# A residual kept in DRAM through the up-projections and the second mixer, its place used for split weights, and one more seven-product unit

## The chip, the cores and the metric

The kernel runs on one core of a Trainium2 chip. The metric is the device time of one execution in microseconds (us); less is better. The engines of the core work side by side, each on its own instructions in order: TensorE (PE) multiplies matrices, VectorE (DVE) and ScalarE (ACT) work element by element, GpSimd (POOL) copies and issues DMAs, SyncE (SP) issues DMAs. Semaphores make one engine wait for another.

## What is computed

A small encoder of two layers on 256 tokens with 2048 channels, in float32. Each layer is a token mixer and a gated MLP with a short convolution; the first layer's mixer is grouped-query attention with rotary positions (A), the second's is dilated sliding-window attention in three head groups (B).

```python
D_MODEL, SEQ, DEPTH, D_FF = 2048, 256, 2, 5632

def conv_ffn(h, w_up, conv_w, conv_b, w_down):
    u = h @ w_up
    ...
    gate, val = jnp.split(u, 2, axis=-1)
    return (jax.nn.silu(gate) * val) @ w_down

def reference(x, a_w_qkv, a_w_o, a_q_gain, a_k_gain, b_w_qkv, b_w_o, rel_bias,
              mix_norm, ffn_norm, w_up, conv_w, conv_b, w_down, final_norm):
    h = x
    for i in range(DEPTH):
        hn = rms_norm(h, mix_norm[i])
        j = i // N_MIXERS
        if i % N_MIXERS == 0:
            h = h + mixer_a(hn, a_w_qkv[j], a_w_o[j], a_q_gain[j], a_k_gain[j])
        else:
            h = h + mixer_b(hn, b_w_qkv[j], b_w_o[j], rel_bias)
        h = h + conv_ffn(rms_norm(h, ffn_norm[i]), w_up[i], conv_w[i], conv_b[i], w_down[i])
    return rms_norm(h, final_norm)
```

`h` is the residual: it is needed for the norm at the start of a sub-layer and for the addition at its end, and not in between.

## The kernel before

**Products.** Every weight matrix is cut into blocks of 512 rows (a group, `kg`) by 512 columns. A weight tile `raw` is half of such a block, [128, 2, 512], 512 KB, loaded by SP. To keep float32 precision, a product is made of three matmuls: ACT rounds `raw` to a high part `wh` (line 147), DVE subtracts it to get a low part `wl` (line 148), and PE multiplies high by high, high by low and low by high (lines 135 to 137). `feed` (line 117) does one block: two splits, and 4 row tiles x 2 token halves x 3 = 24 matmuls of 512 columns. `project` (line 160) does one column block of all groups. `wh` and `wl` have four buffers each (`NHL`), `raw` has four, and in some stages every third `raw` comes from one or two more places (`extra`, line 102).

**Seven-product units.** For some groups `fast_unit` (line 167) computes the four quarter products of two column blocks with seven products in place of eight, by Strassen's method. It loads four weight tiles, makes four sums of them on DVE (line 181), splits seven tiles (lines 182 and 183) and runs 7 x 6 = 42 matmuls (lines 189 to 191), where two fed blocks would take 48. The seven results go to seven or eight accumulators; `fold` (line 196) or the end of `up_pair` (line 525) adds them up on DVE. In an up-projection, pair `p` of a gate and a value block goes through `up_pair` when `p` is in `UP`: six fed blocks and one unit, for group 0. The combinations of the inputs that a unit needs (`picks`) are made once for a layer, at the end of pair 0 (`sums`, line 521).

**Stages.** Mixer A, MLP of layer 0, mixer B, MLP of layer 1. An MLP runs in two halves (`HALVES`: pairs 0 to 5, then 6 to 10). Each half first makes its pairs of up-projections, then adds its part of the down-projection to `h`: in the first half by two calls of `pair` (line 216) for the column blocks (0, 1) and (2, 3); in the second half column block 0 alone, then `pair` for (1, 2), then block 3. `pair` runs fed blocks and units in the order it is given; its `finish` adds one side to `h` (`add_residual`, line 461), and the generator `closing` adds the folds to `h` and calls `post` for each column block, where there is one. Mixer B projects two halves of heads (`hf`) for three groups each, some of them by `up_pair` (`MIX`), then the values, and ends in `out_proj` (line 894), which uses `project2` for the column blocks (0, 1) and `pair` for (2, 3).

**The residual.** `h` (line 58) is one tile [128, 2, 2048] on chip, 16 KB in each partition, for the whole run. After the last addition to a column block, `post` takes its sum of squares (`sumsq_cols`, line 368) and starts `late_transpose` (line 403), which turns the block into the inputs `hT` of the next sub-layer: transpositions on DVE, copies on POOL and ACT, splits on ACT and DVE.

**What sets the order.** Work beside the products is written as generators, which `step` (line 85) advances between blocks. The order of the text is a priority only: a scheduler orders each engine's instructions by priority and by when their inputs and buffers are free, and `tc.high_priority(offset=AHEAD)` raises the splits by 60 places. POOL issues its DMAs in the order of its own instructions; SP issues all weight loads. The output is scaled by `put` and written by `send` (lines 810 to 853) at the very end, first for the first token half, then for the second.

## Time and profile before

| | us |
|---|---|
| median of three runs | 2223.42 |
| lowest and highest of them | 2221.92, 2224.94 |
| span of the profiled execution, first to last instruction | 2220.5 |
| PE busy | 2207.1 |
| DVE busy | 1823.1 |
| ACT busy | 1528.2 |
| POOL busy | 546.1 |

Of the profiled execution the span is known, and no time of its own beside it. The mean granted clock of PE is 0.999 of full speed. The shares of busy time are means over stages of different kinds; for one stage the view of busy times by stretches is read. Stages in the trace, by the first matmul of each: the MLP of layer 0 from about 257 us, its first down-projections from 517, its second half from 643, mixer B from 964, the MLP of layer 1 from 1506, the output from 2210. In a row, PE is a matmul, DVE, ACT and POOL are those engines, "q" behind an engine is its queue; L148 is line 148; `wl<-raw,wh` is the tile written and the tiles read; x7 is a count. In the timeline the columns are the start, the duration, the engine, the line, the operation and, in brackets, the idle time before it and what ended it.

### The profile page before, as it was taken

The numbers are of one execution on the slowest core, as the hardware profiler recorded it, in microseconds if no ns is written. First come the engines' busy times: TensorE is split into PE (matmuls) and PEld (weight loads), VectorE is DVE, ScalarE is ACT, GpSimd is POOL, SyncE is SP. The second block draws the span as 40 slices with busy tenths as digits, with TensorE's granted clock in tenths as the row PEclk, the third lists the DMA queues.
The fourth block names the chain that finished last, engine by engine and source line by source line (L and its number), as shares of the span: only waits on it lengthen the run. The fifth ranks groups of instructions, "written<-read, shape, count | busy, mean of one in ns | idle before, by whom it ended". The sixth has DMA issues, their size and how long they took to land.

```text
span 2220.5 us, 28992 instructions
## 1 busy us (share of the span) xinstructions
PE 2207.1 (99%) x9933; PEld 1828.5 (82%) x9933; DVE 1823.1 (82%) x2295; ACT 1528.2 (69%) x2328; POOL 546.1 (25%) x793
## 2 busy tenths in 40 slices
PE   9999999999999999999999999999999999999998
PEld 7888888888888888888888888888888888888887
DVE  6877669899897998868876878587798998879887
ACT  7666677787457787677756775567777855678764
POOL 3343222321003221042354216003222300212211
PEclk9999999999999999999999999999999999999999
DMA  8665665656656566665666555556555565656754
GB/s 305 192 220 184 216 188 190 201 189 196 203 181 222 186 205 200 204 202 195 183 199 199 174 180 189 190 184 214 181 202 194 192 209 190 217 162 218 224 193 143
DMA packets 126181, 439.60 MB, mean 198 GB/s; under 512 B 14408, under 2 KB 18248, under 8 KB 126032
## 3 DMA queue, kind: packets, MB, share of 16 engines
q1 hardware_dynamic: 123056, 429.05, 59.2%
q0 software_dynamic: 2688, 8.39, 1.5%
q8 instruction: 78, 1.28, 0.2%
q14 instruction: 71, 0.58, 0.1%
q10 hardware_dynamic: 288, 0.30, 0.0%
HBM read 432.34 MB, written 5.34 MB: 197 GB/s over the span
## 4 chain that ended last, share of the span: by engine, by line
PE 54%; POOL 1%; issue 1%; DMA 0%; ACT 0%; DVE 0%; POOLq 0%; DVEq 0%; ACTq 0%
PE acc L136 15%; PE acc L135 15%; PE acc L137 15%; PE ps L190 1%; PE ps L189 1%; PE ps L191 1%; PE acc L190 1%; PE acc L189 1%; PE acc L191 1%; DMA raw<-in_w_b_dram 0%; POOL wide L399 0%; PE ps L1422 0%; PE ps L342 0%; POOL wide L384 0%; ACT wh L147 0%
## 5 line engine op out<-in xcount | busy, mean ns | idle before, releaser
L148 DVE TENSOR_TENSOR wl<-raw,wh 128x1024 fp32r<-128x1024 f32 (+1 forms) x700 | 858.9, 1237 | 257.6 <-ACT wh L147 253.1
L147 ACT ACTIVATE wh<-raw 128x1024 fp32r<-128x1024 f32 (+1 forms) x700 | 726.8, 1046 | 342.5 <-PE acc L137 240.6
L136 PE MATMUL acc<-wl,xh 128*128 128x512 f32 x1984 | 773.8, 390 | 1.5 <-DVE wl L148 1.4
L135 PE MATMUL acc<-wh,xh 128*128 128x512 f32 x1984 | 773.7, 390 | 0.5 <-ACT wh L147 0.5
L137 PE MATMUL acc<-wh,xh 128*128 128x512 f32 x1984 | 772.1, 389 | 0.0
L136 PEld LDWEIGHTS acc<-wl,xh 128*128 128x128 f32 x1984 | 372.6, 188 | 81.5 <-DVE wl L148 5.7
L135 PEld LDWEIGHTS acc<-wh,xh 128*128 128x128 f32 x1984 | 372.5, 188 | 77.4 <-ACT wh L147 1.0
L137 PEld LDWEIGHTS acc<-wh,xh 128*128 128x128 f32 x1984 | 372.4, 188 | 76.9
L632 POOL COPY u<-quad 32x256 f32<-32x256 f32 x352 | 237.7, 675 | 702.5 <-DVE quad L380 684.4
L135 PE MATMUL acc<-wh,a 128*128 128x512 f32 x720 | 280.9, 390 | 0.0
L136 PE MATMUL acc<-wl,a 128*128 128x512 f32 x720 | 280.3, 389 | 0.0
L137 PE MATMUL acc<-wh,a 128*128 128x512 f32 x720 | 280.0, 389 | 0.0
L182 ACT ACTIVATE wh<-raw 128x1024 fp32r<-128x1024 f32 x140 | 148.5, 1061 | 122.4 <-PE acc L137 102.6
L183 DVE TENSOR_TENSOR wl<-raw,wh 128x1024 fp32r<-128x1024 f32 x140 | 166.9, 1218 | 6.3 <-ACT wh L182 5.8
L632 ACT ACTIVATE u<-quad 32x256 f32<-32x256 f32 x352 | 147.8, 420 | 23.2 <-DVE quad L380 18.7
L137 PEld LDWEIGHTS acc<-wh,a 128*128 128x128 f32 x720 | 135.1, 188 | 28.3 <-DVE a L331 0.2
L135 PEld LDWEIGHTS acc<-wh,a 128*128 128x128 f32 x720 | 135.2, 188 | 27.7
L136 PEld LDWEIGHTS acc<-wl,a 128*128 128x128 f32 x720 | 135.2, 188 | 27.6 <-DVE wl L148 0.3
L399 POOL COPY wide<-quad 32x256 f32<-32x256 f32 x88 | 54.8, 622 | 234.8 <-DVE quad L380 167.8
L492 ACT ACTIVATE stg<-acc,rstd 128x512 f32<-128x512 f32 x122 | 81.9, 685 | 32.9 <-PE acc L137 21.3
L384 POOL COPY wide<-quad 32x256 f32<-32x256 f32 x133 | 89.8, 675 | 41.4 <-DVE quad L380 32.0
L380 DVE STREAM_TRANSPOSE quad<-stg 128x512 f32<-128x512 f32 x112 | 75.7, 696 | 11.6 <-ACT stg L492 11.4
(318 smaller groups left out, 2444.5 us busy)
## 6 DMA issues: line engine op xcount, KB each, us to landing
raw<-in_w_up_dram SPq DMA_DIRECT2D x352, 512.0 KB, 4.6
raw<-in_w_down_dram SPq DMA_DIRECT2D x176, 512.0 KB, 4.6
raw<-in_w_b_dram SPq DMA_DIRECT2D x144, 512.0 KB, 4.6
raw<-in_w_bo_dram SPq DMA_DIRECT2D x48, 512.0 KB, 4.4
raw<-in_w_a_dram SPq DMA_DIRECT2D x40, 512.0 KB, 4.7
raw<-in_w_ao_dram SPq DMA_DIRECT2D x32, 512.0 KB, 4.5
raw<-in_w_a_dram SPq DMA_DIRECT2D x16, 256.0 KB, 5.8
there<-quad POOLq DMA_DIRECT2D x6, 512.0 KB, 3.7
```

Source lines behind the costliest of these rows:

```text
L135: nc.tensor.matmul(accs[m], xh, wh[:, j, :], start=st, stop=False)
L136: nc.tensor.matmul(accs[m], xh, wl[:, j, :], start=False, stop=False)
L137: nc.tensor.matmul(accs[m], xl, wh[:, j, :], start=False, stop=sp)
L147: nc.scalar.activation(wh[:, c], r[:, c], AF.Copy)
L148: newest[0] = nc.vector.tensor_tensor(wl[:, c], r[:, c], wh[:, c].bitcast(F32), ALU.subtract)
L182: nc.scalar.activation(wh, r, AF.Copy)
L183: newest[0] = nc.vector.tensor_tensor(wl, r, wh.bitcast(F32), ALU.subtract)
L380: nc.vector.transpose(quad[:, :, at, :], src.rearrange("p (x c t) -> p c x t", c=4, t=32))
L384: nc.gpsimd.tensor_copy(o[32 * c:32 * c + 32, :, 32 * q:32 * q + 32], quad[32 * q:32 * q + 32, c])
L399: nc.gpsimd.tensor_copy(dst, src)
L492: evac[0] = nc.scalar.activation(o[:, m, :], accs[m], AF.Copy, scale=rstd[:, m:m + 1])
L632: put(u[32 * c:32 * c + 32, :, :, 32 * q:32 * q + 32], quad[32 * q:32 * q + 32, c].rearrange("p (j m) t -> p j m t", m=2))
```

## The change

`UP` gets 1 in addition, so that the second pair of the first half goes through `up_pair` in both layers. `h` becomes four tiles of [128, 2, 512], one for a column block, in four places `h0` to `h3`. `put_away` writes a column block to DRAM on the POOL queue and gives up its tile; `fetch` takes a new tile and reads it back. A block is written away when its last addition is done (in the mixers' output, in the first half of both MLPs, and in the second half of the first), and read back before the next addition. While it is away, every third split takes its `wh` and `wl` from the places of `h` (`h0` and `h2`, or `h1` and `h3`, in turn) and not from the four buffers; `more` switches this on from the end of a half's first pair to the end of its last, and in mixer B from the end of its first group to the last but one value projection. `closing` now calls `post` in the first half as well, which there is `put_away`. The writes of the output are cut at the new tiles' borders.

```diff
-UP = 2, 4, 6, 8
+UP = 1, 2, 4, 6, 8
...
-    h = hpool.tile([P, 2, D], F32, name="h")
+    h = {}
...
+    def new_h(n):
+        h[n] = hpool.tile([P, 2, 512], F32, tag=f"h{n}", name=nm("h"))
+        return h[n]
+
+    away, more, splits = {}, [False], [0]
+
+    def put_away(n):
+        if n not in away:
+            away[n] = dpool.tile([P, 2, 512], F32, name=f"away{n}")
+        nc.gpsimd.dma_start(away[n], h.pop(n))
+
+    def fetch(n):
+        if n in h:
+            return
+        nc.gpsimd.dma_start(new_h(n), away[n])
+
+    def new_split():
+        splits[0] += 1
+        i = splits[0] // 3 % 2
+        if more[0] and splits[0] % 3 == 0:
+            return [hpool.tile([P, 2, 512], F32R, tag=f"h{i + k}", name=nm(t)) for k, t in ((0, "wh"), (2, "wl"))]
+        return [spool.tile([P, 2, 512], F32R, tag=t, name=nm(t), bufs=NHL) for t in ("wh", "wl")]
...
@@ feed and fast_unit
-            wh = spool.tile([P, 2, 512], F32R, tag="wh", name=nm("wh"), bufs=NHL)
-            wl = spool.tile([P, 2, 512], F32R, tag="wl", name=nm("wl"), bufs=NHL)
+            wh, wl = new_split()
...
@@ pair
         def closing():
             yield from fold(acc, *ns, *folds())
-            for side in range(2 if post else 0):
+            for side in range(2):
                 yield
                 while side not in added:
                     yield
...
         for i, (kg, side) in enumerate(order):
             while ready is not None and kg not in ready:
                 step()
+            if i == 4:
+                fetch(ns[0])
+                fetch(ns[1])
...
@@ late_transpose
+        src = h[n]
         yield
...
@@ ffn, in the loop over pairs
                     extra[0] = fp, ["raw2"]
+                    more[0] = True
                     start(value_gen(va, value, gate, last_value))
...
+                more[0] = False
                 start(flush(last_value))
...
@@ ffn, post, second half of the first layer
                         sumsq_cols(ss, n, junk)
                         start(late_transpose(hTn, n, g_next, fp, "cg", lambda: quad_tile(fp, "quad", 2)))
+                        put_away(n)
...
@@ ffn, the output
-                    put(0, 0, 1024, "act", r)
-                    put(0, 1024, 1536, "act", r)
-                    send(0, 0, 1024, nc.sync)
-                    send(0, 1024, 2048, nc.sync)
+                    for c in range(0, 1536, 512):
+                        put(0, c, c + 512, "act", r)
+                    for c in range(0, 2048, 512):
+                        send(0, c, c + 512, nc.sync)
...
-                    put(1, 1024, 1536 + NT, "dve", r)
+                    put(1, 1024, 1536, "dve", r)
+                    put(1, 1536, 1536 + NT, "act", r)
...
@@ ffn, the down-projections of the first half
                         pair(wd, ns, slots, both[0] + both[3] + [(4, 0)] + f0 + [(4, 1), (5, 0)] + f1 + [(5, 1)], spot, folds,
-                             None, 3 * (ns[0] == 0), ready)
+                             put_away, 3 * (ns[0] == 0), ready)
...
@@ ffn, the down-projections of the second half
                 for kg in range(np_):
                     while kg not in ready:
                         step()
+                    if kg == 2:
+                        fetch(0)
...
                 pair(wd, (1, 2), slots, order, spot, folds, post, 0, ready)
+                fetch(3)
...
@@ out_proj
         def post(n):
             sumsq_cols(ss, n, junk)
             start(late_transpose(hTn, n, g_next, pool, tag, new_quad))
+            put_away(n)
...
+        for n in range(2):
+            fetch(n)
         if units:
...
@@ mixer_a
             def load_x(n):
-                nc.sync.dma_start(h[:, :, n * 512:(n + 1) * 512],
+                nc.sync.dma_start(new_h(n),
                                   x[:, n * 512:(n + 1) * 512].rearrange("(p m) c -> p m c", m=2))
...
@@ mixer_b
                     start(s_gen(g, project(w_b, ns[1], hT, kgs), kT, bts))
+                    more[0] = True
...
                 for g in range(3):
+                    more[0] = hf == 0 or g < 2
                     accs = project(w_b, 6 * g + 4 + hf, hT, kgs)
```

(The further lines of the diff put `h[n][:, m]` in the place of `h[:, m, n * 512:(n + 1) * 512]`.)

More of the change, by code (lines that the diff above doesn't have):

```diff
@@ L176, in fast_unit @@
         for i, (q, r) in enumerate(((1, b11), (2, b21), (3, b22), (5, t1), (7, b12), (6, t2), (4, t4))):
-            wh = spool.tile([P, 2, 512], F32R, tag="wh", name=nm("wh"), bufs=NHL)
-            wl = spool.tile([P, 2, 512], F32R, tag="wl", name=nm("wl"), bufs=NHL)
+            wh, wl = new_split()
             with tc.high_priority(offset=AHEAD):
@@ L197, in hs @@
         def hs(m, n):
-            return h[:, m, n * 512:(n + 1) * 512]
+            return h[n][:, m]
         tt = nc.vector.tensor_tensor
@@ L369, in sumsq_cols @@
         for m in range(2):
-            nc.scalar.activation(junk(), h[:, m, n * 512:(n + 1) * 512], AF.Square,
+            nc.scalar.activation(junk(), h[n][:, m], AF.Square,
                                  accum_out=ss[:, m, n:n + 1])
@@ L411, in late_transpose @@
             for m in range(2):
-                quad_T(quad, slice(m, 8, 2), h[:, m, n * 512:(n + 1) * 512])
+                quad_T(quad, slice(m, 8, 2), src[:, m])
             yield
@@ L422, in late_transpose @@
         space, quad_tag, wide_tag = next_space[0]
-        src = h[:, :, n * 512:(n + 1) * 512]
         quad, o = quad_tile(space, *quad_tag), wide_tile(space, *wide_tag)
@@ L462, in add_residual @@
         for m in range(2):
-            hs = h[:, m, n * 512:(n + 1) * 512]
+            hs = h[n][:, m]
             nc.vector.tensor_tensor(hs, accs[m], hs, ALU.add)
@@ L782, in post @@
                         for m in range(2):
-                            hs = h[:, m, n * 512:(n + 1) * 512]
+                            hs = h[n][:, m]
                             nc.scalar.activation(junk(), hs, AF.Square, accum_out=ss[:, m, n:n + 1])
@@ L808, in ffn, with cols @@
                 outv = out.rearrange("(p m) c -> m p c", m=2)
+                def cols(m, c0, c1):
+                    return h[c0 // 512][:, m, c0 % 512:(c1 - 1) % 512 + 1]
                 def put(m, c0, c1, how, r):
-                    hs = h[:, m, c0:c1]
+                    hs = cols(m, c0, c1)
                     if how == "fin":
@@ L819, in send @@
                 def send(m, c0, c1, eng):
-                    eng.dma_start(outv[m, :, c0:c1], h[:, m, c0:c1])
+                    eng.dma_start(outv[m, :, c0:c1], cols(m, c0, c1))
                 def first_out(acc):
-                    hs = h[:, 0, 1536:]
+                    hs = h[3][:, 0]
                     nc.vector.tensor_tensor(hs, acc, hs, ALU.add)
@@ L827, in first_out @@
                     put(0, 1536, 2048, "fin", r)
-                    put(0, 0, 1024, "act", r)
-                    put(0, 1024, 1536, "act", r)
-                    send(0, 0, 1024, nc.sync)
-                    send(0, 1024, 2048, nc.sync)
+                    for c in range(0, 1536, 512):
+                        put(0, c, c + 512, "act", r)
+                    for c in range(0, 2048, 512):
+                        send(0, c, c + 512, nc.sync)
                 def last_out(acc, parts):
-                    hs = h[:, 1, 1536:]
+                    hs = h[3][:, 1]
                     nc.vector.tensor_tensor(hs, acc, hs, ALU.add)
```

## The prediction

> **What bounds the kernel now.** I read the page first: the share of each engine, then the list of who waited for whom, then the timeline of PE alone.
>
> ```profile
> span 2220.5 us, 28992 instructions
> PE 2207.1 (99%) x9933; PEld 1828.5 (82%) x9933; DVE 1823.1 (82%) x2295; ACT 1528.2 (69%) x2328; POOL 546.1 (25%) x793
> ACT wh L147 <- PE acc L137: 240.6, 177, 2.1
> DVE wl L148 <- ACT wh L147: 253.1, 221, 3.8
> 1900.06 0.39 PE L137 MATMUL acc<-wh,xh 128*128 128x512 f32 x1
> ...
> 1905.95 0.39 PE L136 MATMUL acc<-wl,xh 128*128 128x512 f32 x1
> ```
>
> PE is busy for 99% of the span, so it is the bound. The timeline gives its pace: the two rows are 26 matmuls apart, (1905.95 - 1900.06) / 26 = 0.2265 us from start to start; the 0.39 is a modelled duration that overlaps the next one. The two waits say the rest: ACT (high parts, line 147) waits 240.6 us for PE to free a split buffer, and DVE (low parts, line 148) waits 253.1 us for ACT. The conversion mostly runs as far ahead as its four buffers allow and stands there. Only two things can then shorten the kernel: fewer matmuls, or the few places where PE waits for a low part. I looked for those as start-to-start distances over 0.227 in the stages where the change gives more split buffers:
>
> ```profile
> 377.79 0.39 PE L135 MATMUL acc<-wh,xh 128*128 128x512 f32 x1
> 378.68 0.50 PE L136 MATMUL acc<-wl,xh 128*128 128x512 f32 x1 [0.50 <-DVE wl L148]
> 487.05 0.39 PE L135 MATMUL acc<-wh,xh 128*128 128x512 f32 x1
> 487.50 0.50 PE L136 MATMUL acc<-wl,xh 128*128 128x512 f32 x1
> 1030.31 0.39 PE L189 MATMUL ps<-wh,s 128*128 128x512 f32 x1
> 1030.72 0.50 PE L190 MATMUL ps<-wl,s 128*128 128x512 f32 x1
> 1282.86 0.39 PE L189 MATMUL ps<-wh,s 128*128 128x512 f32 x1
> 1283.17 0.50 PE L190 MATMUL ps<-wl,s 128*128 128x512 f32 x1
> 1735.90 0.39 PE L135 MATMUL acc<-wh,xh 128*128 128x512 f32 x1
> 1736.25 0.50 PE L136 MATMUL acc<-wl,xh 128*128 128x512 f32 x1
> ```
>
> They lose 0.89 - 0.23 = 0.66, then 0.22, 0.18, 0.08 and 0.12 us: 1.26 us in all. So the buffers can win about 1.3 us at most, in a kernel of 2220.
>
> **The change, part by part.**
>
> *The unit.* With 1 in UP, pair 1 of the first half goes through up_pair in both layers. Two projections are 2 x 4 groups x 24 = 192 matmuls; six fed groups and a unit of 7 x 6 are 144 + 42 = 186. That is 6 fewer per layer, 12 in all, on the path: 12 x 0.2265 = **-2.72 us**. What it adds lies on DVE and ACT, and the same unit one pair later (340 to 382 us) shows its price; a view by stretches gives the room (columns: length, PE, PEld, DVE, ACT, POOL busy, clock, DMA share, GB/s).
>
> ```profile
> 296.00:340.00 44.00, 44.00 (x196) 36.44 (x195) 29.32 (x38) 35.90 (x55) 14.97 (x24) 1.00 0.62 189
> 340.00:382.00 42.00, 41.50 (x183) 33.72 (x182) 37.06 (x43) 31.07 (x47) 9.11 (x12) 1.00 0.54 178
> 426.00:468.00 42.00, 42.00 (x187) 34.75 (x187) 37.10 (x40) 31.01 (x44) 8.88 (x15) 1.00 0.58 198
> 468.00:512.00 44.00, 43.94 (x194) 35.91 (x193) 42.06 (x63) 36.42 (x58) 14.62 (x18) 1.00 0.60 196
> L183 DVE TENSOR_TENSOR wl<-raw,wh 128x1024 fp32r<-128x1024 f32 x7 | 8.2, 1218 | 0.0
> L181 DVE TENSOR_TENSOR raw<-raw,raw 128x1024 f32<-128x1024 f32 x4 | 4.9, 1225 | 0.1
> L551 DVE TENSOR_TENSOR acc<-acc,junk 128x512 f32<-128x512 f32 x1 | 0.7, 690 | 0.0
> L182 ACT ACTIVATE wh<-raw 128x1024 fp32r<-128x1024 f32 x7 | 7.4, 1059 | 4.9 <-PE acc L137 4.4 <-PE ps L191 0.3 <-PE acc L191 0.2
> 374.19 2.01 ACT L147 ACTIVATE wh<-raw 128x1024 fp32r<-128x1024 f32 x2 [3.77 <-DMA raw<-in_w_up_dram]
> ```
>
> Splits go from 16 to 12 + 7 = 19. DVE gets 3 x 1.22 + 4 sums x 1.23 + 8 folds of about 0.69 = 14.1 us; ACT gets 3 x 1.06 + about 0.7 = 3.9 us. In pair 1 (296 to 340) DVE has 44 - 29.3 = 14.7 us free and ACT 8.1. It fits, but DVE is then nearly full, and no lead is built for pair 2. The unit's burst shows in pair 2: PE lost 0.66 us at 378, since ACT waited 3.77 us for a weight tile whose buffer the unit held (last row). More split buffers do not mend that. For pair 1 I bound it by 0, as in the unit of pair 4 (426 to 468, PE 42.00 of 42.00), and by 0.66 in both layers, 1.32 in all. I take half: **+0.66 us**; the range keeps both ends, with -0 below, since an added burst cannot give time back.
>
> *Split buffers in h's place.* Every third split takes one of two more pairs, so four become six in the up-projections and the second mixer. Pair 5 (468 to 512), where DVE is busy for 42.06 of 44 us, gets the lead that pair 4 can now build; its losses at 487 and 1736 and those of the second mixer at 1030 and 1283 should go: 0.22 + 0.12 + 0.18 + 0.08 = **-0.60 us**, bounded by 0 and by all 1.26. What is late next at these places is DVE itself, which then has its work done earlier.
>
> *The residual's journeys.* Per use of put_away and fetch, n from 0 to 3: twenty writes and twenty reads of 512 KB, 21 MB beside 439.60. They are issued on POOL and share the DMA engines with the weights.
>
> ```profile
> there<-quad POOLq DMA_DIRECT2D x6, 512.0 KB, 3.7
> raw<-in_w_down_dram SPq DMA_DIRECT2D x176, 512.0 KB, 4.6
> 97.40 0.64 POOL L1171 DMA_DIRECT2D there<-quad  x1 [1.04 <-DVE mx L1121]
> 3.53 0.52 POOL L1236 DMA_DIRECT2D rb<-in_rel_bias_dram  x1
> 520.47 4.81 POOL L632 COPY u<-quad 32x256 f32<-32x256 f32 x8 [12.76 <-DVE quad L380]
> 631.63 0.11 POOL L603 MEMSET u<- 128x4 f32 x1 [106.34 <-DVE wl L183]
> 0.00:50.00 50.00, 47.78 (x200) 38.43 (x201) 32.57 (x47) 37.24 (x65) 15.63 (x31) 1.00 0.92 322
> ```
>
> Issue costs POOL 40 x 0.64 = 26 us; POOL is idle for 75% of the span, so nothing of it is on the path. A write goes ahead of the copies of the same late transposition on POOL; these must wait for two DVE transpositions first, which covers 0.64 us; without that cover the start of a stage would be 0.64 us later. What waits *behind* a fetch on POOL? In the first halves nothing: POOL idles from 525.3 to 631.6 (two rows above). The order on an engine is not that of the text: the load at line 1236, written in a generator that starts in pair 1, ran at 3.53 us. I expect each fetch likewise as soon as PE has freed h's place, near the end of the up-projections, some 20 us or more before the sums need it. The writes cannot move: they follow the last addition to h, and fall on the weights of the next unit.
>
> ```profile
> 587.39 0.68 DVE L214 TENSOR_TENSOR h<-h,fold 128x512 f32<-128x512 f32 x1
> 586.89 7.87 SPq L170 DMA_DIRECT2D raw<-in_w_down_dram  x4
> 599.04 1.23 DVE L181 TENSOR_TENSOR u<-raw,raw 128x1024 f32<-128x1024 f32 x1 [2.37 <-DMA raw<-in_w_down_dram]
> 610.41 1.23 DVE L183 TENSOR_TENSOR wl<-raw,wh 128x1024 fp32r<-128x1024 f32 x1
> 613.42 0.39 PE L190 MATMUL ps<-wl,s 128*128 128x512 f32 x1
> ```
>
> The last addition to h's columns 0 to 1023 ends at 588.1, and the four weight tiles of the next unit are issued from 586.9 to 594.8. DVE already waited 2.37 us for them. The fastest stretch moved 322 GB/s, so 512 KB take 0.524 / 0.322 = 1.63 us, two transfers 3.26. The slack behind them: the low part finished at 611.64 is used at 613.42, 1.78 us later. One transfer in the way is hidden; two would cost 3.26 - 1.78 = 1.48 us. There are five such places (the second pair and the next half's first unit in each layer; the pair in the second mixer's output). From 0 to 5 x 1.48 = 7.4 us; as the share of 0.6 of the DMA engines in the stretches above leaves 40% free, I stay near the lower end: **+0.60 us**. A gain is excluded: bytes are only added.
>
> The Trainium skill, "DMA: Bandwidth & Descriptors", section "Issuing engines are not separate DMA queues", says that transfers started by different engines run on the same 16 engines and interleave. By that the POOL queue is no separate road, and the upper end would be the sum; no run so far has a large POOL transfer beside a unit, so this trace cannot confirm it.
>
> *The output.* Two sends become four, and one multiplication is cut in two.
>
> ```profile
> 2214.82 1.01 DVE L817 TENSOR_SCALAR h<-h,rstd 128x512 f32<-128x512 f32 x2 [0.67 <-POOL rstd L805]
> 2214.82 0.72 ACT L815 ACTIVATE h<-h,rstd 128x512 f32<-128x512 f32 x1 [3.28 <-POOL rstd L805]
> ```
>
> DVE hands a third of its second piece to ACT, which is done first. I put it at 0, bounds -0.3 (a third of 1.01) and +0.4 (half of the 0.72, if ACT ends last).
>
> **Sum**: -2.72 - 0.60 + 0.66 + 0.60 = -2.06 us. The profiled execution spans 2220.5 us, so its span becomes 2218.4. Of that execution only the span is known; the median of the runs is 2223.42, 2.9 us above it, which I take for what lies around the span. Forecast: 2223.42 - 2.06 = **2221.4 us**, 0.09% less. A measurement of this kernel tells about 0.2% (4.4 us) from no change; this is not.
>
> **The rivals.**
>
> *Everything goes well* (faster). The unit costs nothing, all 1.26 us of losses go, the output gains 0.3, and the transfers hide: 2223.42 - 2.72 - 1.26 - 0.3 = 2219.1; a little more lead elsewhere in the stages brings it below the bound of 2219.0. For it: the conversion waits 240 us for buffers. Against it: the loss at 378 is a weight tile's. Chance 0.2.
>
> *Vector work takes the unit's gain back* (no change). Pairs 1 and 2 follow each other with a unit each, and DVE has 0.6 us left in pair 1. If both pairs lose 0.66 in both layers where only one did, 4 x 0.66 = 2.64 replaces 0.66: 2223.4. For it: the rows of pair 1. Against it: the six buffers, and 4.9 us of free DVE time in pair 2. Chance 0.2.
>
> *The writes hold up the next unit* (slower). Two 512 KB writes come between a unit's weight tiles at the five places; from 1.78 us of delay on it reaches PE. Price 7.4 in place of 0.6: 2228.2; with no slack at all, 5 x 3.26 = 16.3 us, 2237.1. For it: DVE's wait of 2.37 us at 599. Against it: free DMA time. Chance 0.1. The page's rule above is this mechanism.
>
> *The buffers do nothing*, since the weight tiles or ACT limit the lead: only the 0.60 is missing, 2222.0, inside the forecast.
>
> The forecast itself has 0.5, spread over about 2219 to 2224. Most of the chance lies within 0.2%. Faster by more: 0.20, from the first rival and a little noise. Slower: 0.11. Within: 0.69. The range takes the bounds -2.72 - 1.26 - 0.3 with another 2 us for what a new order of instructions may move, and the first end of the slower rival: 2217.0 to 2228.2.
>
> **What would show it.** PE has 9933 - 12 = 9921 matmuls. DVE's busy time grows by about 28 us, ACT's by 8, the POOL queue's bytes from 8.39 to 29.4 MB. The distances at 487, 1030, 1283 and 1736 shrink to 0.23; a new one at a unit near 320 us shows the price of pair 1. DVE's wait for a weight tile near 599 (2.37) grows by 1 to 2 us and PE's distances there stay at 0.23. The forecast is wrong if PE waits for low parts behind the writes, if something on POOL stands behind a fetch for long, or if the first matmuls of a stage come later than before.

## The result, and the profile after

The changed kernel takes 2235.42 us (median of four runs, 2234.39 to 2235.83), the kernel before 2223.59 in the same comparison: a ratio of 1.0052 with an interval of 1.0039 to 1.0065. It is about 11.6 us slower, and the time lies above the predicted range of 2217.0 to 2228.2. The profiled execution took 2235.83 us for a span of 2234.1; in all profiled runs from here on the time is 1.7 to 2.1 us above the span.

The page of the changed kernel: the span, the engines, and three rows of its list of transfers (count, size, median us from issue to landing).

```profile
span 2234.1 us, 29129 instructions
PE 2210.2 (99%) x9921; PEld 1827.9 (82%) x9921; DVE 1844.9 (83%) x2325; ACT 1527.7 (68%) x2338; POOL 562.7 (25%) x833
...
raw<-in_w_b_dram SPq DMA_DIRECT2D x144, 512.0 KB, 4.7
...
away<-h POOLq DMA_DIRECT2D x20, 512.0 KB, 5.5
h<-away POOLq DMA_DIRECT2D x20, 512.0 KB, 6.4
```

PE has the 9921 matmuls that were predicted and is still the bound, yet the span grew by 13.6 us. So PE must wait more often, and the list of waits (who waited for whom, us in all, times, longest) says where the conversion stands. First before, then after:

```profile
ACT wh L147 <- PE acc L137: 240.6, 177, 2.1
...
ACT wh L147 <- DMA raw<-in_w_up_dram: 21.7, 8, 4.3
...
ACT wh L147 <- DMA raw<-in_w_b_dram: 11.9, 6, 3.4
```

```profile
ACT wh L169 <- PE acc L160: 177.0, 135, 2.1
ACT wh L169 <- DMA raw<-in_w_up_dram: 30.7, 21, 3.7
ACT wh L169 <- DMA raw<-in_w_b_dram: 29.7, 15, 4.4
```

More buffers did what they promise: ACT waits 64 us less for PE to free one. In return it stands longer in front of weight tiles that are not there yet (33.6 us before, 60.4 after). Standing there is harmless unless something urgent is queued behind it.

To find the places I measured each stage from its first matmul to the first of the next. All runs of the study are in the table, in us. "Pairs 1-5" is what these stages last beyond 43.52 us for a plain pair and 42.16 for one with a unit (their lengths where PE does not wait), in layer 0 and 1 (in layer 0 four small matmuls of the bias table lie in pair 2 too, so 1.00 there is the least, and no loss); "down" is the first call of `pair` in the first half of each layer; "B start" is the last column block of the first MLP and group 0 of mixer B; "B values" the values of its first half; "2nd" the losses of pairs 6 to 10 of both layers; "end" the time from the last matmul to the end of the span.

```
                 mixer A  pairs 1-5     down          B start  B values  2nd   end
before            250.79  2.27  0.69   63.19  62.59    71.43    70.41   0.36  7.53
changed           253.23  1.57  1.95   66.95  64.18    77.70    71.77   0.00  9.06
e1_unit_alone     251.09  4.46  3.35   62.81  62.56    71.20    70.41   0.41  7.53
e2_no_unit        252.49  1.00  0.00   63.19  63.12    75.24    71.67   0.00  9.05
e3_no_places      250.84  4.23  3.44   62.77  62.59    71.15    70.41   0.16  9.05
e4_tiles_only     252.38  1.80  0.43   62.56  63.21    71.65    70.41   0.30  7.38
e5_mixer_b_plain  250.33  1.00  0.77   65.57  62.59    71.87    70.41   0.00  9.06
e6_later_places   253.67  1.59  0.35   66.67  63.37    72.31    71.81   0.00  9.05
e7_two_units      251.26  1.55  0.06   62.73  63.05    75.75    72.03   0.00  9.06
e8_spaced_units   250.98  2.63  1.84   67.46  67.55    71.55    70.41   0.40  7.40
e9_first_halves   253.12  1.00  0.00   63.67  62.60    71.23    70.41   0.18  7.40
e10_sums_on_pool  253.63  5.91  7.04   64.93  64.10    71.11    70.41   5.11  7.40
e11_pool_sums     252.37 12.18 11.36   62.87  62.92    71.46    70.41   5.11  7.40
e12_by_act        250.60  4.40  3.25   62.63  62.56    70.72    70.41   4.01  7.41
e13_less_sums     251.41  2.91  1.47   63.77  63.37    71.30    70.41   0.00  7.40
e14_changed_less  252.57  1.00  0.00   63.49  62.80    76.99    72.15   0.00  9.06
e15_units_apart   251.02  1.34  0.42   62.56  63.03    71.45    70.41   0.38  7.40
e16_apart_six     253.00  1.00  0.00   63.73  62.69    71.20    70.41   1.49  7.40
```

The program of mixer A is the same in all but for the tiles of `h`, yet its time differs by up to 3 us between the profiled executions (see the last section), so it is left out when kernels are compared by stages. For the changed kernel the other columns give: the unit's 12 matmuls -2.72, pairs 1 to 5 +0.56, down +5.35, B start +6.27, B values +1.36, pairs 6 to 10 -0.36, the end +1.53; that is 12.0 us. Mixer A adds 2.44 and other stages of mixer B take off 0.6, together 13.8, within 0.3 of the 13.6 by which the span grew. Three places had not been foreseen: the start of mixer B, the first down-projections, and the end.

**The start of mixer B.** The timeline of the changed kernel, first POOL's writes and then DVE:

```profile
944.84 0.54 POOL L76 DMA_DIRECT2D away<-h  x1 [48.16 <-DVE h L232]
947.94 0.53 POOL L76 DMA_DIRECT2D away<-h  x1 [2.56 <-DVE h L235]
```

```profile
951.15 1.30 DVE L404 STREAM_TRANSPOSE quad<-h 128x512 f32<-128x512 f32 x2
956.32 1.23 DVE L170 TENSOR_TENSOR wl<-raw,wh 128x1024 fp32r<-128x1024 f32 x1 [3.88 <-DMA away<-h]
957.86 1.23 DVE L170 TENSOR_TENSOR wl<-raw,wh 128x1024 fp32r<-128x1024 f32 x1 [0.30 <-ACT wh L169]
961.09 1.22 DVE L170 TENSOR_TENSOR wl<-raw,wh 128x1024 fp32r<-128x1024 f32 x1 [2.01 <-ACT wh L169]
```

And ACT, with a row of the list of waits below it:

```profile
954.38 1.06 ACT L169 ACTIVATE wh<-raw 128x1024 fp32r<-128x1024 f32 x1 [4.40 <-DMA raw<-in_w_b_dram]
...
DVE wl L170 <- DMA away<-h: 4.2, 2, 3.9
```

The split at 954.38 (high part) and 956.32 (low part) goes into `h`'s place, so it belongs to a later group. It came up early on both queues, presumably because its place looked free while the four other buffers were taken; no view shows the scheduler's reason. Its high part stands on ACT for 4.40 us, because its weight tile has not landed. Its low part stands on DVE for 3.88 us, until the write issued at 947.94 has landed. The two waits overlap: the high part ends at 955.44, and before that DVE could not have begun, so the write adds 0.9 us to this wait. Both engines stand in the one stretch where they also have to turn `h` into the next inputs, and everything behind is late. The same stretch by transfers:

```profile
raw<-in_w_b_dram SPq DMA_DIRECT2D x5, 512.0 KB, 6.5
raw<-in_w_down_dram SPq DMA_DIRECT2D x2, 512.0 KB, 6.2
away<-h POOLq DMA_DIRECT2D x2, 512.0 KB, 8.5
```

Mixer B's weight tiles took a median of 6.5 us between 940 and 960 us, 4.7 over the whole run (4.5 in the same stretch of the kernel before), and the writes 8.5. The rule of the Trainium skill that the prediction weighed ("DMA: Bandwidth & Descriptors", "Issuing engines are not separate DMA queues") agrees with these rows. Two possible causes are thus in one place: the early split in the queue, and the traffic.

**The first down-projections.** The timeline of PE in the changed kernel:

```profile
547.71 0.39 PE L210 MATMUL acc<-wh,s 128*128 128x512 f32 x1
549.90 0.50 PE L211 MATMUL acc<-wl,s 128*128 128x512 f32 x1 [1.80 <-DVE wl L204]
...
550.50 0.63 PE L210 MATMUL acc<-wh,s 128*128 128x512 f32 x1
550.92 0.63 PE L211 MATMUL acc<-wl,s 128*128 128x512 f32 x1
551.35 0.63 PE L212 MATMUL acc<-wh,s 128*128 128x512 f32 x1
```

PE waits for a low part at the first unit (549.90 - 547.71 = 2.19 in place of 0.23), and for about eight matmuls behind it the pace is 0.427 us, not 0.2265, which costs another 1.6 us. DVE is behind there, 30 us into the down-projections, where there should be time enough.

### The profile page after: what moved, and what is told of

The parts are those of the page before. It is cut to its first block, busy times and chain, and to the rows that moved or that the text cites. A ratio compares the mean times of both kernels' runs of the same rounds, so it can differ in the third digit from the quotient of the medians.

```text
span 2234.1 us, 29129 instructions
## 1 busy us (share of the span) xinstructions
PE 2210.2 (99%) x9921; PEld 1827.9 (82%) x9921; DVE 1844.9 (83%) x2325; ACT 1527.7 (68%) x2338; POOL 562.7 (25%) x833
## 3 DMA queue, kind: packets, MB, share of 16 engines
q8 instruction: 77, 1.26, 0.2%
## 4 chain that ended last, share of the span: by engine, by line
PE 80%; DVE 8%; DMA 3%; ACT 3%; issue 3%; POOL 2%; SPq 0%; DVEq 0%; POOLq 0%; ACTq 0%
PE acc L159 23%; PE acc L160 22%; PE acc L158 22%; DVE wl L170 3%; PE ps L210 2%; PE ps L211 2%; PE ps L212 2%; DVE wl L204 1%; PE acc L211 1%; PE acc L212 1%; PE acc L210 1%; DMA raw<-in_w_b_dram 1%; ACT wh L169 1%; DMA raw<-in_w_up_dram 1%; POOL u L656 1%
## 5 line engine op out<-in xcount | busy, mean ns | idle before, releaser
L170 DVE TENSOR_TENSOR wl<-raw,wh 128x1024 fp32r<-128x1024 f32 (+1 forms) x692 | 842.5, 1232 | 238.8 <-ACT wh L169 230.8
L169 ACT ACTIVATE wh<-raw 128x1024 fp32r<-128x1024 f32 (+1 forms) x692 | 711.5, 1045 | 305.6 <-PE acc L160 177.0
L159 PE MATMUL acc<-wl,xh 128*128 128x512 f32 x1952 | 762.3, 391 | 4.1 <-DVE wl L170 4.0
L158 PE MATMUL acc<-wh,xh 128*128 128x512 f32 x1952 | 762.2, 391 | 2.3 <-ACT wh L169 2.3
L160 PE MATMUL acc<-wh,xh 128*128 128x512 f32 x1952 | 760.2, 389 | 0.0
L158 PEld LDWEIGHTS acc<-wh,xh 128*128 128x128 f32 x1952 | 366.9, 188 | 78.6 <-ACT wh L169 3.4
L160 PEld LDWEIGHTS acc<-wh,xh 128*128 128x128 f32 x1952 | 366.9, 188 | 76.2
L203 ACT ACTIVATE wh<-raw 128x1024 fp32r<-128x1024 f32 x154 | 161.9, 1059 | 132.9 <-PE acc L160 95.1
L204 DVE TENSOR_TENSOR wl<-raw,wh 128x1024 fp32r<-128x1024 f32 x154 | 188.0, 1234 | 19.9 <-ACT wh L203 18.8
L76 POOL DMA_DIRECT2D away<-h x20 | 10.7, 537 | 380.0 <-DVE h L232 253.2
L516 ACT ACTIVATE stg<-acc,rstd 128x512 f32<-128x512 f32 x122 | 80.4, 682 | 36.1 <-DVE acc L580 15.7
L408 POOL COPY wide<-quad 32x256 f32<-32x256 f32 x133 | 84.9, 638 | 43.8 <-DVE quad L404 34.8
L202 DVE TENSOR_TENSOR raw<-raw,raw 128x1024 f32<-128x1024 f32 x70 | 87.9, 1256 | 1.3 <-DMA raw<-in_w_up_dram 0.4
```

The source lines that it names most:

```text
L158: nc.tensor.matmul(accs[m], xh, wh[:, j, :], start=st, stop=False)
L159: nc.tensor.matmul(accs[m], xh, wl[:, j, :], start=False, stop=False)
L160: nc.tensor.matmul(accs[m], xl, wh[:, j, :], start=False, stop=sp)
L169: nc.scalar.activation(wh[:, c], r[:, c], AF.Copy)
L170: newest[0] = nc.vector.tensor_tensor(wl[:, c], r[:, c], wh[:, c].bitcast(F32), ALU.subtract)
L202: nc.vector.tensor_tensor(*sums[q], ALU.add)
```

## The experiments

**First the parts.** Four kernels divide the change. The theories are named in the expectations by letters: H, T, U, O.

e1, the kernel before with the unit alone; e2, the changed kernel without it:

```diff
-UP = 2, 4, 6, 8
+UP = 1, 2, 4, 6, 8
```

> Of the change only the seven-product unit of pair 1 (UP begins with 1), in the kernel before: h stays one tile on chip. The prediction's own terms give -2.72 +0.66 = -2.06 us. Theory H (splits in h's place stand at the head of DVE's and ACT's queues and wait for a write) and theory T (the 21 MB compete with the weight tiles) both leave the unit innocent: 0.5 to 3.5 us less than before. Theory U (DVE has no room for the unit's sums and folds): no gain, or some us more than before.

> The changed kernel without the unit of pair 1 (UP as before): the journeys, the split buffers in h's place and the cut output stay. If the parts add up, the unit's own difference is taken away: H and T: 12 to 16 us more than before. U: about the time before.

e3, no split in `h`'s place (`more` is always false); e4, in addition no unit and no journeys:

```diff
     def put_away(n):
-        if n not in away:
...
-        nc.gpsimd.dma_start(away[n], h.pop(n))
+        return
...
-                    more[0] = True
+                    more[0] = False
```

> The changed kernel in which no split uses h's place (more is never true): the unit, the four h tiles, all forty journeys and the cut output stay. H: the start of mixer B loses no 6 us and the pairs of the first halves come near their old length; the time falls to within 3 us of the time before. T: the same bytes move at the same places, so 9 us or more of the 11.8 remain.

> Neither unit nor journeys nor split buffers: h is four tiles that stay on chip, and the output is cut into the changed kernel's pieces. H and T: within 1 us of the time before. Theory O (the scheduler's new order, through the smaller h tiles and the cut output alone, makes the loss): 3 us or more above it, with the output's end 1.6 us later, as in the changed kernel.

Measured: e4 0.9992 of the time before (0.9983 to 1.0001), e1 1.0012 (1.0003 to 1.0021), e2 1.0015 (1.0007 to 1.0024), e3 1.0024 (1.0015 to 1.0033). O falls: tiles and output alone cost nothing. The parts do not simply add up: e1 is 3.0 us over before by the medians, but leaving the unit out of the changed kernel (e2) takes away 8. U is right that the unit costs more than it gains, and wrong that it is all, since e2 is slower than before too. T falls in its main point: e3 has all forty transfers at the same places, and in the table its stages are those of e1 within 0.25 us, but for the end. (The profiled execution of e3 is its fastest; by the medians e3 is 2.5 us above e1, of which the end is 1.5.) H is right that the places cost time in mixer B: its start is 71.15 in e3, with the writes and without the places, and 75.24 in e2, with both. H is wrong for the first halves and for the time of e3: pairs 1 to 5 stay as long as in e1, and e3 is 5.5 us over before, not within 3. The end of 9.05 goes with the journeys (e2, e3), not with the output (e4).

**Mixer B.** e5 uses no places in mixer B; e6 begins with them only at the values of its first half:

```diff
                     start(s_gen(g, project(w_b, ns[1], hT, kgs), kT, bts))
-                    more[0] = True
+                    more[0] = hf == 1
```

> The changed kernel in which the second mixer's splits never use h's place (more stays false there); all forty journeys, the unit and the places in the up-projections stay. H (a split in h's place stands at the head of DVE's queue and waits for a write): the losses of the changed kernel at the end of the first MLP (0.86), in group 0 of mixer B (5.41) and in its first values (1.35) go, 6 to 8 us in all: 2227 to 2230. T (bytes beside the weight tiles): the same writes fall on the same weights, so it stays within 2 us of the changed kernel's 2235.4.

> The changed kernel in which the second mixer begins to use h's place only with the values of its first half, over 100 us after the writes. H: only the waiting for the write goes, so group 0 of mixer B and the end of the first MLP come back (6.3 us: about 2229), while the 1.35 us in the first values, where six buffers let ACT stand before a weight tile, stay. If six buffers as such cost time in the mixer, about half of the 7.6 stays.

Measured: e5 1.0018 (1.0009 to 1.0027), e6 1.0018 (1.0009 to 1.0027). In both, the start of mixer B is back (71.87 and 72.31 in place of 77.70) although the writes still fall there: not the bytes alone, but the early splits in `h`'s place, made the loss. The timeline of DVE in e6 at the same place:

```profile
952.01 1.30 DVE L404 STREAM_TRANSPOSE quad<-h 128x512 f32<-128x512 f32 x2
954.27 1.33 DVE L170 TENSOR_TENSOR wl<-raw,wh 128x1024 fp32r<-128x1024 f32 x1 [0.96 <-ACT wh L169]
956.88 0.89 DVE L361 SCALAR_TENSOR_TENSOR xh<-wide,gain,xh 128x256 fp32r<-128x256 f32 x2 [1.28 <-ACT xh L358]
```

No split waits for a write any more, and the next inputs (line 361) come at 956.88, 15.9 us after the start of the last column block; in the changed kernel the first came at 962.23, after 21.7. (Before it was 15.7.)

H's reason, the wait for a write, explains only a part. Of all kernels here, only the changed one and e14 have splits of DVE that wait for a write (3.88 and 3.1 us at this place). In e2, and in e7 below, none does, yet the start of mixer B lasts 75.24 and 75.75 us, 3.8 and 4.3 over before; in e2 the next inputs come after 19.8 us. ACT in e2:

```profile
945.63 1.06 ACT L169 ACTIVATE wh<-raw 128x1024 fp32r<-128x1024 f32 x1 [1.94 <-DMA raw<-in_w_b_dram]
...
953.57 2.01 ACT L169 ACTIVATE wh<-raw 128x1024 fp32r<-128x1024 f32 x2
955.48 1.69 ACT L358 ACTIVATE xh<-wide,gain 128x256 fp32r<-128x256 f32 x4
```

Splits stand for a weight tile, and run, ahead of the next inputs (line 358). In e2 eight matmuls at half pace (last section) make up 1.6 of the 3.8 us; in e7 none does. So 4.3 of the 6.3 us can come without any wait for a write, and about 2 are left for it, as far as single executions tell.

The 1.4 us of the values stay in e6 (71.81) and go in e5 (70.41), as H said. There it is ACT that stands in front of a tile, in the changed kernel (first ACT, then PE):

```profile
1161.87 1.06 ACT L169 ACTIVATE wh<-raw 128x1024 fp32r<-128x1024 f32 x1 [3.62 <-DMA raw<-in_w_b_dram]
1163.27 1.06 ACT L169 ACTIVATE wh<-raw 128x1024 fp32r<-128x1024 f32 x1 [0.34 <-DMA raw<-in_w_b_dram]
1164.24 0.36 ACT L354 ACTIVATE a<-ps 128x256 fp32r<-128x256 f32 x1
```

```profile
1164.48 0.39 PE L160 MATMUL acc<-wh,xh 128*128 128x512 f32 x1
1165.98 0.39 PE L368 MATMUL ps<-pT,vh 128*128 128x256 f32 x1 [1.11 <-DVE a L355]
```

Two splits that have a buffer but wait for their weight tile stand ahead of the copy of line 354, for which DVE and then PE wait. Before, a missing buffer kept the splits back and the copy came in time.

**Where the unit's cost comes out.** e7 takes the unit of pair 4 out of the changed kernel; e8 puts three units into pairs 1, 3 and 5 of e4:

```diff
-UP = 1, 2, 4, 6, 8
+UP = 1, 2, 6, 8
```

> The changed kernel with UP = 1, 2, 6, 8: the unit of pair 1 stays, that of pair 4 is left out, so that the first halves have two units as before. Theory D (a unit eats 4 to 7 us of the conversion's lead, DVE has too little free time to win it back before the next one, and the debt is paid where the down-projections begin): pairs 3 to 5 win the lead back, the losses of 3.76 and 1.59 us at the first down-projections go, +2.72 us for the two units less: about 2.5 us less than the changed kernel. Theory F (the fetches of h take the DMA engines from the weights at that place): those losses stay and the time is 2.7 us more than the changed kernel's.

> h as four tiles on chip, no journeys, no places, and UP = 1, 3, 5, 6, 8: three units in the first half, no two of them in neighbouring pairs. If only neighbouring units hurt, each costs at most the 0.66 us seen at a unit before: 1 to 3 us less than before, near 2221. D in its stricter form (the lead is spent wherever DVE is nearly full, pairs 3 and 5 with 42 of 44 us busy): losses in pair 5 and at the first down-projections, so no gain or up to 4 us more than before.

Measured: e7 1.0025 (1.0016 to 1.0034), e8 1.0035 (1.0022 to 1.0048). In e7 the losses at the first down-projections are gone (62.73 and 63.05): F falls, the fetches are the same. Against before, the gain is about 6 us and not 2.5 as D expected, since the pairs and the start of mixer B are shorter too. e8 has no neighbouring units and is still worse: 67.46 and 67.55 there, 9 us over before by the medians, where D's stricter form allowed 4. The cost is a debt: it appears where the next unit meets a conversion that has no lead left, be it in pair 2 (e1, e3), or two stages later.

The lead can be read directly: the time between the end of a low part and the matmul that first uses it. At the first block of pair 1, on entering the unit of pair 2, at that unit's least, and on entering the first unit of the down-projections, in layer 0:

```
                    pair 1   pair 2's unit   its least   down, first unit
before                5.82        4.48          0.11          3.55
e1_unit_alone         5.82        0.76          0.05          3.52
e2_no_unit           11.31        8.30          3.31          3.02
changed              11.31        7.11          0.91          1.14
e14_changed_less     11.31        7.28          1.81          2.75
```

(Pair 2's unit is the first of the layer in before and e2, and the second in the others.) Six buffers double the lead, and two units in a row eat nearly all of it. DVE's timeline in e1, in the unit of pair 2, shows why; below it PE's:

```profile
359.74 1.21 DVE L181 TENSOR_TENSOR raw<-raw,raw 128x1024 f32<-128x1024 f32 x1
360.87 1.21 DVE L183 TENSOR_TENSOR wl<-raw,wh 128x1024 fp32r<-128x1024 f32 x1
362.01 1.21 DVE L181 TENSOR_TENSOR raw<-raw,raw 128x1024 f32<-128x1024 f32 x1
363.14 1.21 DVE L183 TENSOR_TENSOR wl<-raw,wh 128x1024 fp32r<-128x1024 f32 x1
364.28 1.21 DVE L181 TENSOR_TENSOR raw<-raw,raw 128x1024 f32<-128x1024 f32 x1
365.41 1.21 DVE L183 TENSOR_TENSOR wl<-raw,wh 128x1024 fp32r<-128x1024 f32 x1
```

```profile
364.41 0.50 PE L190 MATMUL ps<-wl,s 128*128 128x512 f32 x1 [0.60 <-DVE wl L183]
...
366.68 0.50 PE L190 MATMUL ps<-wl,s 128*128 128x512 f32 x1 [0.63 <-DVE wl L183]
```

DVE works without a gap, one operation each 1.13 us. A unit has eleven, 4 sums and 7 splits: 12.4 us, while PE needs 42 x 0.2265 = 9.5. In its middle each product needs a sum and a split, 2.27 us, and that is PE's distance too (366.68 - 364.41).

**Taking the unit's sums away.** e10 (places and journeys in the first halves only, which is e9, with the unit) and e11 (tiles on chip, with the unit) give two of the four sums to POOL; e13 (as e11) and e14 (the changed kernel) leave them out. The edits reach every unit that goes through `up_pair`, the four of mixer B too:

```diff
-                    nc.vector.tensor_tensor(*sums[q], ALU.add)
+                    (nc.gpsimd if spot is None and q in (5, 6) else nc.vector).tensor_tensor(*sums[q], ALU.add)
```

```diff
-                if q in sums:
+                if q in sums and not (spot is None and q in (5, 6)):
```

> The kernel of e9 with the unit of pair 1, and in the units of the up-projections two of the four sums of weight tiles run on POOL. D (DVE's time is what a unit costs): 2.5 us less of DVE for each unit, the loss at the first down-projections (3.8 and 1.6 us in the changed kernel) is under 1 us, and the time 1 to 3 us below e9's. If a sum on POOL comes too late for the unit (2.2 to 3.9 us by POOL's rows of 512 columns, in place of 1.23), PE waits inside the units and it is 2 us or more above e9's.

> h as four tiles on chip, no journeys, no places, the unit of pair 1, and the same two sums on POOL. The unit alone lost 2.3 and 2.6 us in pairs 2 to 4. D: that falls by half or more, so the time is within 1 us of the tiles alone. If latency inside the unit counts with four buffers, not DVE's time, the loss stays or grows.

> h as four tiles on chip, the unit of pair 1, and two of the four sums of weight tiles left out in the units of the up-projections and of the second mixer's projections; nothing takes their place. D: a unit then takes DVE 9 x 1.13 = 10.2 us in place of 11 x 1.13 = 12.4, against 9.5 us of PE, so the 2.3 and 2.6 us lost in pairs 2 to 4 fall under 0.8, and the time is 1 to 4 us less than before. If weight tiles or ACT set the unit's pace, the losses stay above 1.5 us each.

> The changed kernel with the same two sums left out in the same units. D: the debt at the first down-projections (3.76 and 1.59 us) falls under 1 us in all, the 6 to 8 us of mixer B stay (H): about 2229 to 2231. If the debt there comes from the fetches of h, it stays: 2234 or more.

Measured: e10 1.0104 (1.0091 to 1.0118), e11 1.0130 (1.0116 to 1.0143): much slower, and no answer to the question: a sum takes 3.0 us on POOL, 1.2 on DVE, and POOL's sums held up DVE itself (last section). e13 0.9998 (0.9989 to 1.0007), e14 1.0019 (1.0010 to 1.0029). Without the sums, pairs 1 to 5 of e13 lose 2.91 and 1.47, in place of 4.46 and 3.35 in e1; in the expectation's terms, pairs 2 to 4 are 0.98 and 0.99 us longer than before, where e1 had 2.28 and 2.60. That lies between the two forecasts (under 0.8, over 1.5), nearer to D. Of what remains in layer 0, 0.8 us lie at 378, as in the kernel before, where a weight tile is late, and 1.0 in one wait for a low part inside the unit of pair 2. The first down-projections of e13, 63.77 and 63.37, are 1.4 us longer than before in sum; kernels without an added unit lie between 62.56 and 63.73 there, so this cannot be told from their spread. In e14 the first down-projections are at 63.49 and 62.80: the debt there is gone, 4.8 of 5.35 us, and pairs 1 to 5 are as good as with no unit. So DVE's time is the unit's price, most clearly with six buffers (e14) and less so with four (e13). Mixer B keeps its loss in e14 (76.99 and 72.15), as H expected. The time, 2227.07, is 2 us below what was expected, since pairs 1 to 5 gained 2.5 us as well.

**The journeys' own price.** e9 keeps the places for the first halves alone, so that 16 transfers remain, without the unit; e12 is e3 with all journeys issued by ACT:

```diff
-        nc.gpsimd.dma_start(away[n], h.pop(n))
+        nc.scalar.dma_start(away[n], h.pop(n))
...
-        nc.gpsimd.dma_start(new_h(n), away[n])
+        nc.scalar.dma_start(new_h(n), away[n])
```

> Only what the runs so far found harmless: h's place is used by the up-projections of the two first halves alone, so that h is put away after each mixer and fetched in the first down-projections (16 transfers on POOL in place of 40), and UP is as before. H: no split waits in mixer B, the gains of e2 in the first halves stay (1.3 us in layer 0, 0.7 in layer 1): 1 to 3 us less than before. Theory E (POOL's last instruction, a drain, lasts 0.08 us longer for each transfer POOL has issued; 54 transfers end it before SP's last wait): the end of the program is as short as before, the drain 5.1 us, in place of 7.05 with an end 1.5 us later.

> The kernel of e3 (unit, forty journeys, no places) with all journeys issued by ACT in place of POOL. E: POOL's drain is back at 3.8 us and the program's end at 7.4 us behind the last matmul in place of 9.05, so 1.5 us less, unless ACT's splits stand behind a write that waits for the last addition to h; then PE loses time at the starts of units. If the late end came from the DRAM traffic itself, it stays at 9.05.

Measured: e9 1.0000 (0.9991 to 1.0008), e12 1.0021 (1.0012 to 1.0031). e9 was expected 1 to 3 us below before, and is not: its pairs 1 to 5 are 2.0 us shorter, but the time is the same (in its profiled execution mixer A is 2.3 us longer). E holds in both: a drain at POOL's end lasts 3.78 us in kernels where POOL issues 38 transfers (e12 among them), 5.09 with 54 (e9) and 7.05 with 78, which is 0.082 us for each. It starts 1.2 us behind the last matmul, and SP is done 6.6 us behind it, so up to some 20 more transfers are hidden and forty are not: the end is 7.40 in e9 and 7.41 in e12, 9.05 in e3. In e12 that gain is lost again: 4.01 us in pairs 6 to 10, most of it in the units of pair 6, 11 to 14 us behind ACT's writes. The list of waits of e12 has splits on ACT that wait for a write, 13.7 us in four waits; each of them stands behind a fetch, which has to wait for the write before it. Whether late weight tiles add to that was not tried.

**Units apart.** e15 is e4, and e16 is e9, with `UP = 1, 4, 6, 8`:

> h as four tiles on chip, no journeys, UP = 1, 4, 6, 8: as many units as before, in pairs 1 and 4 in place of 2 and 4, two plain pairs between them. D: no debt is left when the next unit comes; the 0.66 us lost in pair 2 before goes, 0.5 to 2 us less than before. If a unit costs about the same wherever it is, no difference beyond 0.5 us to the tiles alone.

> The kernel of e9 (h's place used in the first halves alone, 16 transfers) with UP = 1, 4, 6, 8. D: all losses of the first halves go and stay away, 1 to 3 us less than before and no more than e15. If the transfers cost more than the places win, it is e15 or above.

Measured: e15 0.9996 (0.9987 to 1.0005), e16 1.0001 (0.9992 to 1.0009). The losses of pairs 1 to 5 are at or near 1.00 and 0.00, but there is nothing beyond that to win: e16 was expected 1 to 3 us below before and is not, and e15 (1.4 us under before by the medians) does not differ from e4 (1.25 under) by the 0.5 us that would have spoken for D. No kernel here beats the one before by more than the measurement can tell; e4, e13 (which leaves work out) and e15 come nearest.

## Why the prediction was wrong, step by step

- **The unit, -2.72**: right as a count. 9921 matmuls, and pair 1 lasts 42.16 us in both layers, with no new distance near 320, where one was expected.
- **Its burst, +0.66, bounds 0 and 1.32**: the first step that failed, by its size. In e1 pairs 1 to 5 lose 7.81 us where they lost 2.96, +4.85; in the changed kernel it is +0.56 there and +5.35 at the first down-projections. The forecast priced a weight tile that comes late behind a unit, at 378. In e1 that place loses 0.2 us; the loss is three waits for low parts inside the unit of pair 2, about 0.8 us each, in both layers. The rival "vector work takes the unit's gain back" named the mechanism and priced it at half. DVE's added work was counted rightly (27.6 us in e1, forecast 28). The error is in the kind of number: 14.7 us of free DVE time in pair 1 is a mean over a stage, while the unit needs 12.4 us of DVE in 9.5 us of PE at once. The 0.66 came from a kernel in which a unit enters with 4 to 6 us of lead and runs down to 0.1 to 0.9.
- **Split buffers, -0.60, bounds 0 and -1.26**: right in kind, and beyond its bound. In e2 all losses of the pairs are gone: 1.27 and 0.69 us in pairs 1 to 5 and 0.36 in pairs 6 to 10, 2.3 in all. The five places that were counted, 1.26, were not all.
- **What the same edit adds**: the second step that failed, by an omission. The prediction put the places in mixer B at a gain and asked only what stands behind a fetch on POOL; it never asked what stands behind a *split* in `h`'s place, which can come up early on the queues of ACT and DVE and there waits for its weight tile or for a write. In mixer B this cost 6.3 us at the start and 1.4 us, by ACT, in the values; e5, without the places there, loses neither. Of the 6.3 us about 2 are left for the wait for a write, by e7. Ten splits of the changed kernel are the first in a place that a write frees, but its list of waits has only two that stood for one.
- **The journeys on the next unit's weights, +0.60**: wrong place. DVE's wait near 599, said to grow by 1 to 2 us, is unchanged (the timeline of DVE in the changed kernel):

```profile
602.79 1.22 DVE L202 TENSOR_TENSOR u<-raw,raw 128x1024 f32<-128x1024 f32 x1 [2.47 <-DMA raw<-in_w_down_dram]
```

  2.47 for 2.37. What the journeys are seen to cost is 1.5 us at the very end, in POOL's drain. The early fetches were harmless, as forecast: with six buffers and without the unit (e2), the first down-projection lasts 63.19 us in layer 0 as before, and 63.12 in layer 1 (62.59).
- **The output, 0**: right; e4 ends 7.38 us behind the last matmul, 7.53 before.
- **From span to time**: the profiled execution of before took about 2222.3 us (2220.5 and 1.8 around it), 1.1 below its median. That moves nothing.

Not settled: the medians of e3 and e5 lie 2.4 and 2.6 us above their profiled executions. With a lead near zero the debt comes out larger in one execution than in another (62.59 to 64.18 us and 65.57 to 66.95 for the same stages in e5 and the changed kernel); which of it makes the difference no run shows.

## What to carry to other kernels

Where a bound engine lives on a lead that others build, count the lead, not the shares: how many operations a new piece of work puts on the feeding engine within its own stretch, against what PE takes for it, and how long the stages behind it need to win that back. An additional buffer lets work come up earlier, and a place that a DMA has to free is not free when it looks so: find the first instruction that uses it on each in-order queue, what it waits for, and what stands behind it. And work moved to an idle engine still has a price: it can take longer there, and it can hold up another engine.

## What the runs showed of the hardware

**POOL and DVE exclude each other on such sums.** The timeline of e10, POOL and then DVE:

```profile
360.76 3.24 POOL L202 TENSOR_TENSOR raw<-raw,raw 128x1024 f32<-128x1024 f32 x1
366.70 2.48 POOL L202 TENSOR_TENSOR raw<-raw,raw 128x1024 f32<-128x1024 f32 x1 [2.69 <-issue]
```

```profile
361.68 2.61 DVE L722 TENSOR_TENSOR a<-cv,a 128x256 fp32r<-128x256 f32 x1
...
366.88 3.37 DVE L204 TENSOR_TENSOR wl<-raw,wh 128x1024 fp32r<-128x1024 f32 x1
```

POOL's sum runs from 360.76 to 364.00, and a DVE operation begun within it, which takes 0.38 us elsewhere, ends at 364.29; the split begun at 366.88 lasts 3.37 us, to 1.07 us behind the end of POOL's second sum, about its own length. The Trainium skill, "SBUF — State Buffer", section "SBUF: two separate sides", describes the port pair of the two engines as an exclusive lock, also against a DVE operation with two inputs in SBUF: these rows agree.

**Half pace after a short gap.** Behind the gap of 2.19 us at 547.71 PE ran about eight matmuls at 0.427 us. Mixer A has a gap of 2.0 to 2.3 us near 142 us in all 18 profiled executions; in 8 of them 5 to 8 matmuls at 0.427 follow, 0.6 to 1.4 us after the gap's end, and all 8 have one of the longer times for mixer A (252.4 to 253.7; one execution, e4, is as long without it). The Trainium skill, "TensorE: Matmul & The Clock Gate", Part 1, gives a free-running idle window of about 3.4 us for the fall to half rate; here a gap of 2.0 to 2.3 us from start to start, 1.8 to 2.0 of it idle, was enough, though not each time.

**POOL's drain** at the end of the program grows by 0.082 us for each transfer that POOL has issued: 3.78, 5.09 and 7.05 us for 38, 54 and 78.
